# Half of a gate product moved into the opening of an RWKV-7 scan, with the scan's first loads reordered

## The chip, the cores and the metric

The kernel runs on 1 core of one Trainium2 chip. The metric is the device time of one execution in microseconds. Lower is better.

## The reference

Two encoder layers on x (512 tokens, 1024 channels, float32). Each is a half-step SwiGLU feed-forward, a token mixer, and another half-step feed-forward, with a layer norm after each. Layer 0 mixes by neighbourhood attention, layer 1 by bidirectional RWKV-7. Only the second mixer matters here:

```
xr, xw, xk, xv, xa, xg = (x + xx * mix[i] for i in range(6))
r = xr @ w_rkv[0];  k = xk @ w_rkv[1];  v = xv @ w_rkv[2]
decay, a = low-rank functions of xw and xa, one per direction
g = sigmoid(xg @ g1) @ g2                      # 1024 -> 160 -> 1024
state_t = state * w_t + (state a_t) b_t + v_t k_t ;  y_t = state r_t      # 16 heads of 64, both directions
out = ((groupnorm(y) + bonus) * g) @ w_out
```

## The kernel before, in words

Everything is laid out with channels (or tokens) on 128 partitions. Products that need accuracy are made of three float32r passes (`mm3`, lines 226 to 230: high x high, high x low, low x high); a product given plain float32 tiles is a single call.

**rwkv_project** (lines 582 to 750) makes the mixer's inputs. Near its end it opens the first scan pool (`scan.begin`), makes the decays of both directions, and the gate: `rank(0)` and `rank(0, g1b)` are g1's product in plain float32 (line 614), tanh makes the sigmoid, `split` cuts it into high and low halves `gh`. Then, for each of eight chunks of 128 output channels, six float32r passes (`mm3` for 128 and for 32 rows of g2), a copy by ACT (`store`, line 643) and a store into the DRAM tile `g` (line 644). Between the chunks runs `scan.front(0, 0)`, the preparation of head pair 0 in the forward direction.

**Scan** works through eight pairs of heads in slots -2 to 7. A slot holds generator threads, and the string `SEQ[n]` says in which order their steps are written: f0, f1 are `front` of a direction (decay sums, line 1266; exponents; rank product; tanh; then DVE's products into ar and bk), g0, g1 `grams` (line 1324, masked by DVE at 1329, with swaps by DMA at 1336 and 1337), t0, t1 `tails`, v `values` (weights wv loaded at line 1356, then eight products with xv, two matmul halves each by `wide`, line 1015), r `receptances`, l `load`, i, k, j the inversion, c the chain over the chunks of time (lines 1474 to 1494), d outputs, b bonus. PE, ACT and DVE keep exactly this order (`manual_schedule(MANUAL_SCAN)`). SP, which issues all DMAs, and POOL are put in order by a scheduler from when each instruction would be ready; after that every queue runs in order.

**receptances** (lines 1083 to 1120) loads the eight chunks of xr into the buffers az[2], xs8 and xs9, then the receptance weights of pairs 1, 4, 6, 7 (`WR_FIRST`; the first goes into xs4), with the eight chunks of xv between, then three more weights into vt. The products alternate between the PSUM banks y and m, one buffer each, and are copied into the tiles yt and yh, one buffer each. The loads are written at the first step of r, in slot -2.

The scan's large pool and a second one (`open`, line 1044) lie over the memory of the pools that rwkv_project closes: the rings that hold gh and the copies to be stored, and the weight tiles that hold g2.

Of the kernel before, what the change touches and what calls it, by code (L numbers as in the profile page):

```python
# [10 lines left out]
F32 = mybir.dt.float32  # L11
# [3 lines left out]
AF = mybir.ActivationFunctionType  # L15
# [3 lines left out]
P = 128  # L19
D = 1024  # L20
S = 512
FF = 2816
NF = FF // P
ND = D // P
# [18 lines left out]
CH = 64  # L43
# [15 lines left out]
}  # L59
SEQ = {  # L60
# [11 lines left out]
}  # L72
EARLY = 5
START_TAGS = ("k", "iv", "r", "lw", "kz0", "ar0", "bk0", "a2r", "a2u", "pcs")
EARLY_TAGS = ("kz1", "v", "vr", "qc", "qd", "zs", "qs", "tm")
DECAY = math.exp(-0.5)
GN_EPS = 64e-5
# [22 lines left out]
class Trunk:  # L100
# [481 lines left out]
    def rwkv_project(self, dram, xraw, w_rkv, w1, w2, a1, g1, g2, heads, xs, scan):  # L582

        nc = self.nc
        if True:
# [77 lines left out]
            with self.tc.manual_schedule(engines=MANUAL):  # L663
# [62 lines left out]
                            nc.sync.dma_start(dram["lw"][:, z, t, ws], th)  # L726

                xs.close()
                scan.begin()
                decays(0)  # L730
                scan.fetch(0, 0)
                pg = [rank(0), rank(0, g1b)]
                gn = (P, 32)
                for i, n in enumerate(gn):
                    raw = self.tmp()[:n]
                    nc.scalar.activation(raw, pg[i][:n], AF.Tanh, scale=0.5)
                    nc.vector.tensor_scalar(raw, raw, 0.5, 0.5, ALU.mult, ALU.add)
                    self.split(gh[i][:n, 0, :], gh[i][:n, 1, :], raw)
# [2 lines left out]
                start = scan.front(0, 0)  # L741
                next(start)
                ug = [self.load_rows(g2, 0), self.load_unit(g2[P:, :])]
                for c in range(ND):
                    pp = self.bank()
                    for i, n in enumerate(gn):
                        cs = slice(c * P, c * P + P)
                        self.mm3(pp, ug[i][:n, 0, cs], ug[i][:n, 1, cs], gh[i][:n, 0, :], gh[i][:n, 1, :], i == 0, i == 1)
                    store(dram["g"][:, c, :], pp)
                    next(start, None)  # L750

    def rwkv_out(self, acc, params, lead):
        self.spare.append(self.ring())
# [256 lines left out]
class Scan:  # L1010
# [10 lines left out]
        self.free = list(range(NBUF))  # L1021
        self.taken, self.st, self.py = {}, {}, {}

    def begin(self):

        nc = self.nc
        pool = self.start = self.opened.enter_context(self.k.pool("rws", "right"))
        self.tri = pool.tile([P, 2, P], F32, name="tri")
        self.mask = pool.tile([P, 2, 2, CH], F32, name="mask")
        self.onesb = pool.tile([P, P], F32, name="onesb")  # L1030
        self.ah = pool.tile([P, 2, S], F32R, name="ah")
        ring = self.k.ring(F32)
        raw, *rest = (ring[:, i * S : (i + 1) * S] for i in range(4))
        self.first.update(zip(("e", "e2", "th"), rest))
        for dst, src in ((raw, self.dram["ah"]), (self.tri, self.consts["tri"])):
            nc.sync.dma_start(dst, src)
        load = self.load(0)
        next(load)
        self.k.split(self.ah[:, 0, :], self.ah[:, 1, :], raw)
        next(load)  # L1040
        for n in ("mask", "onesb"):
            nc.sync.dma_start(getattr(self, n), self.consts[n])

    def open(self, pool):

        self.pool = pool
        early = self.early = self.opened.enter_context(self.k.pool("rwe", "right"))
        self.eye = self.consts["eye"]
        self.xv = pool.tile([P, ND, S], F32, name="xv")
        unit = lambda i: (pool.tile([P, 2, 4, 2, CH], F32, name=f"xs{i}"), pool.tile([P, 2, 4, CH], F32, name=f"tb{i}"))  # L1050
        units = {i: unit(i) for i in (2, 4, 3)}
        for n in ("e", "e2", "th"):
            self.place(n, [P, S], 2)
        for n in ("yt", "yh"):
            self.place(n, [P, S])
        self.place("bon", [P, S], 2)
        self.place("gate", [P, S])
        units.update({i: unit(i) for i in (7, 0, 9, 1)})
        self.place("vt", [P, NC, 2, 2, CH], 2)
        units.update({i: unit(i) for i in (5, 6, 8)})  # L1060
        self.units = [units[i] for i in range(NBUF)]


        self.az = [pool.tile([P, 2, NU, CH], F32, name=f"az{i}") for i in range(3)]
        for i in range(2):
            self.clear(i)
        self.room(0)
# [4 lines left out]
    def tile(self, tag, shape, bufs=1, dtype=F32):  # L1072
        if tag in self.first:
            return self.first.pop(tag)
        pool = self.start if tag in START_TAGS else self.early if tag in EARLY_TAGS else self.pool
        return pool.tile(shape, dtype, name=tag, tag=tag, bufs=bufs)

# [5 lines left out]
    def receptances(self):  # L1083

        nc = self.nc
        one = lambda ap: ap.rearrange("p a b c d -> p (a b c d)")
        az = self.az[2].rearrange("p a b c -> p (a b c)")
        xr = [h[:, i * S : (i + 1) * S] for h, n in ((az, 4), (one(self.units[-2][0]), 2), (one(self.units[-1][0]), 2)) for i in range(n)]
        for c in range(ND):
            nc.sync.dma_start(xr[c], self.dram["xr"][:, c, :])  # L1090
        w = {}

        def load(hp, ap):
            w[hp] = ap.rearrange("p (c f) -> p c f", c=ND)
            nc.sync.dma_start(w[hp], self.w_r[:, hp * P : (hp + 1) * P].rearrange("(c p) f -> p c f", p=P))

        for hp, i in zip(WR_FIRST, (4, 5, 6, 7)):
            load(hp, one(self.units[i][0]))
            if hp == 1:
                for c in range(ND):  # L1100
                    nc.sync.dma_start(self.xv[:, c, :], self.dram["xv"][:, c, :])
        rest = [hp for hp in range(1, ND) if hp not in WR_FIRST]
        order = WR_FIRST + tuple(rest)
        while rest:
            pair, rest = rest[:2], rest[2:]
            vt = self.tile("vt", [P, NC, 2, 2, CH], 2)
            for i, hp in enumerate(pair):
                load(hp, one(vt)[:, i * D : (i + 1) * D])
        for i, hp in enumerate(order):
            pr = self.k.bank("ym"[i % 2])  # L1110
            for c in range(ND):
                self.wide(pr, w[hp][:, c, :], xr[c], c == 0, c == ND - 1)
                if c % 2 and c < ND - 1:
                    yield
            t = self.tile(("yh", "yt")[hp % 2], [P, S])
            nc.scalar.activation(t, pr, AF.Copy)
            nc.sync.dma_start(self.dram["rkv"][0][:, hp, :], t)
            if hp == order[-1]:
                self.clear(2)
            yield  # L1120
# [9 lines left out]

    def run(self, late, lead, ln):
        with self.k.tc.manual_schedule(engines=MANUAL_SCAN):
            self.zs = []
            for _ in range(2):
                self.unit()
            self.rs, self.out = self.receptances(), self.outs()
            self.led, self.stored = [], 0
            for n in range(-2, HEADS // 2):
                if n == HEADS // 2 - 1:
                    self.early.tile([P, 56], F32, name="pad")  # L1140
                    self.opened.close()
                    late.enter_context(self.k.early())
                    self.lw = self.leads(lead, ln)
                self.slot(n)
            self.ending = self.finish(HEADS // 2 - 1)
            next(self.ending)
# [59 lines left out]
    def slot(self, n):  # L1206
# [3 lines left out]
            ("t0", "tails", n + 2, 0), ("t1", "tails", n + 2, 1), ("v", "values", n + 2), ("b", "bonus", n + 2),  # L1210
            ("e", "gate", n - 1), ("x", "finish", n - 1), ("n", "turn", n + 1), ("i", "invert", n + 2), ("k", "inverted", n + 1), ("j", "merge", n + 1),
            ("l", "load", n + 3), ("c", "chain", n), ("d", "outputs", n))}
        threads["r"], threads["o"] = self.rs, self.out
        threads["w"] = self.lw if n == HEADS // 2 - 1 else iter(())
        for name in SEQ.get(n, SEQ[0]).split():
# [8 lines left out]
    def load(self, hp):  # L1224

        k, nc, tile_ = self.k, self.nc, self.tile
        p = self.st[hp] = Pair()
        p.k, p.iv = (tile_(n, [P, S], 2) for n in ("k", "iv"))
        nc.sync.dma_start(p.k, self.dram["rkv"][1][:, hp, :])
        for h in range(2):  # L1230
            nc.sync.dma_start(p.iv[HALF[h]], self.dram["iv"][2 * hp + h : 2 * hp + h + 1, :].broadcast_to([CH, S]))
# [21 lines left out]
    def front(self, hp, z):  # L1253
# [2 lines left out]
        p = self.st[hp]  # L1256
        way = slice(None, None, -1) if z else slice(None)
        if z == 0:
            p.r = tile_("r", [P, S], 2)
            nc.sync.dma_start(p.r, self.dram["rkv"][0][:, hp, :])  # L1260
        if (hp, z) not in self.lws:
            self.fetch(hp, z)
# [88 lines left out]
    def values(self, hp):  # L1351

        k, nc, tile_ = self.k, self.nc, self.tile
        p = self.st[hp]
        wv = tile_("wv", [P, ND, P])
        nc.sync.dma_start(wv, self.w_v[:, hp * P : (hp + 1) * P].rearrange("(c p) f -> p c f", p=P))
        yield
        p.v = tile_("v", [P, S], 2)
        pv = k.bank("a")
        for c in range(ND):  # L1360
            self.wide(pv, wv[:, c, :], self.xv[:, c, :], c == 0, c == ND - 1)
            if c < ND - 1:
                yield
        nc.scalar.activation(p.v, pv, AF.Copy)
        yield

    def bonus(self, hp):
        k, nc, tile_ = self.k, self.nc, self.tile
# [379 lines left out]
```

## Time and profile before

| what | us |
|---|---|
| median of 3 runs | 2245.5 (2244.44 to 2251.05) |
| the profiled execution | 2242.69 |
| its span, first to last instruction | 2240.9 |
| PE busy | 2175.0 (97% of the span) |
| POOL, DVE, ACT busy | 1411.7, 1060.0, 958.0 |

The profile follows one execution. Times in its rows are microseconds from the start of the span unless marked ns. PE is TensorE, DVE VectorE, ACT ScalarE, POOL GpSimd, SP the engine that issues DMAs. A DMA row gives the time of its issue, not of its transfer. PE's matmuls overlap, so a row's duration is longer than its distance to the next. What stands in brackets behind a row is the idle time of its engine before it and the instruction or transfer that ended it. The granted clock is the share of TensorE's full 2.4 GHz.

### The profile page before, as it was taken

Reading aid. Unit: us, or ns where it says so; the run is one execution under the profiler, and the core shown is the slowest. Engines: PE = TensorE matmul, PEld = TensorE weight load, DVE = VectorE, ACT = ScalarE, POOL = GpSimd, SP = SyncE. Lnnn points to the kernel's source line nnn. Section 1 sums busy time; section 2 is a strip of 40 time slices with the busy share of each in tenths; the row PEclk is TensorE's granted clock in tenths of the full one; section 3 lists DMA queues with packets and bytes.
Section 4 is the critical chain, followed back from the end, with each engine's and each line's share of the span. In section 5 each row is a group of like instructions: output and inputs, shape, how many; then the busy total and the mean of one; then the engine's idle time right before and its main releaser. Section 6 shows DMA issues by size and latency. Waiting matters only on the chain. (4 is left out here: it accounts for less than half of the span.)

```text
span 2240.9 us, 35205 instructions
## 1 busy us (share of the span) xinstructions
PE 2175.0 (97%) x13850; PEld 1706.6 (76%) x13850; DVE 1060.0 (47%) x1524; ACT 958.0 (43%) x1678; POOL 1411.7 (63%) x1234
## 2 busy tenths in 40 slices
PE   8999999999999999999999999799999899999998
PEld 7888888887888888888888875345666557888886
DVE  2333355377432333633333588234788545333345
ACT  3333345376343333443333444336777533333333
POOL 6877855554488786588787432044676712888754
PEclk9999999999999999999999999899999999999999
DMA  6444462432344444454444546844544643544443
GB/s 200 141 142 150 146 230 97 126 91 88 109 139 142 149 146 160 141 188 141 137 141 141 197 128 214 249 123 130 135 121 118 191 152 98 161 140 137 141 169 122
DMA packets 350497, 328.82 MB, mean 147 GB/s; under 512 B 48458, under 2 KB 277450, under 8 KB 350332
## 3 DMA queue, kind: packets, MB, share of 16 engines
q1 hardware_dynamic: 350332, 326.58, 47.1%
q8 instruction: 109, 1.79, 0.3%
q14 instruction: 56, 0.46, 0.1%
HBM read 262.26 MB, written 47.74 MB: 138 GB/s over the span
## 5 line engine op out<-in xcount | busy, mean ns | idle before, releaser
L224 POOL TENSOR_TENSOR w<-raw,w 128x1024 fp32r<-128x1024 f32 x200 | 492.0, 2461 | 246.5 <-ACT w L223 241.7
L228 PE MATMUL bank<-xT,w 128*128 128x512 f32 x1408 | 549.3, 390 | 0.0
L229 PE MATMUL bank<-xT,w 128*128 128x512 f32 x1408 | 548.0, 389 | 0.0
L230 PE MATMUL bank<-xT,w 128*128 128x512 f32 x1408 | 547.9, 389 | 0.0
L223 ACT ACTIVATE w<-raw 128x1024 fp32r<-128x1024 f32 (+1 forms) x204 | 215.3, 1058 | 329.2 <-POOL ts L794 138.0
L430 DVE SCALAR_TENSOR_TENSOR ar<-bank,tmp 128x512 f32<-128x512 f32 x88 | 60.9, 692 | 583.7 <-PE bank L230 574.7
L230 PEld LDWEIGHTS bank<-xT,w 128*128 128x128 f32 x1408 | 264.3, 188 | 55.0
L228 PEld LDWEIGHTS bank<-xT,w 128*128 128x128 f32 x1408 | 264.3, 188 | 54.0
L229 PEld LDWEIGHTS bank<-xT,w 128*128 128x128 f32 x1408 | 264.4, 188 | 53.6
L823 PE MATMUL bank<-wx,an 128*128 128x512 f32 x792 | 187.3, 389 | 0.0
L1413 POOL TENSOR_TENSOR tm<-qs,zs 128x126 f32<-128x126 f32 (+22 forms) x248 | 104.5, 421 | 115.9 <-DVE qs L1406 66.2
L823 PEld LDWEIGHTS bank<-wx,an 128*128 128x128 f32 x792 | 148.7, 188 | 30.9
L823 PE MATMUL bank<-w,ring 128*128 128x512 f32 x720 | 168.7, 390 | 2.0 <-POOL w L224 2.0
L224 POOL TENSOR_TENSOR wx<-ra,wx 128x512 fp32r<-128x512 f32 x132 | 166.8, 1291 | 3.1 <-ACT wx L223 3.1
L224 DVE TENSOR_TENSOR ring<-ar,ring 128x1024 fp32r<-128x1024 f32 x44 | 129.5, 2943 | 75.5 <-ACT ring L223 75.4
L823 PEld LDWEIGHTS bank<-w,ring 128*128 128x128 f32 x720 | 135.0, 188 | 31.2 <-POOL w L224 2.9
L428 ACT ACTIVATE tmp<-bank 128x512 f32<-128x512 f32 x88 | 52.6, 598 | 229.2 <-PE bank L230 229.1
L224 POOL TENSOR_TENSOR ring<-raw,ring 128x1024 fp32r<-128x1024 f32 x28 | 68.4, 2449 | 103.6 <-ACT ring L223 98.9
L1415 POOL TENSOR_TENSOR zs<-zs,tm 128x126 f32<-128x126 f32 (+22 forms) x248 | 112.9, 455 | 19.4
L223 ACT ACTIVATE wx<-ra 128x512 fp32r<-128x512 f32 x132 | 82.9, 633 | 72.0 <-PE bank L823 67.9
L224 POOL TENSOR_TENSOR w<-late,w 128x1024 fp32r<-128x1024 f32 x30 | 75.3, 2511 | 60.0 <-ACT w L223 59.9
L228 PE MATMUL bank<-xT,ring 128*128 128x256 f32 (+1 forms) x352 | 102.1, 298 | 5.0 <-ACT ring L223 2.2
(295 smaller groups left out, 3752.1 us busy)
## 6 DMA issues: line engine op xcount, KB each, us to landing
raw<-in_ffn_w_in_dram SPq DMA_DIRECT2D x176, 512.0 KB, 3.9
ra<-in_ffn_w_out_dram SPq DMA_DIRECT2D x44, 1024.0 KB, 5.0
late<-d_late SPq DMA_DIRECT2D x34, 512.0 KB, 5.4
late<-in_ffn_w_out_dram SPq DMA_DIRECT2D x28, 512.0 KB, 4.4
raw<-in_w_qkv_dram SPq DMA_DIRECT2D x24, 512.0 KB, 3.9
d_late<-ts SPq DMA_DIRECT2D x44, 256.0 KB, 3.4
d_late<-ra SPq DMA_DIRECT2D x44, 256.0 KB, 2.0
xs<-ar SPq DMA_DIRECT2D x64, 128.0 KB, 2.4
```

What stands on the lines that cost most here:

```text
L223: self.hi = self.nc.scalar.activation(h, raw, AF.Copy).ins
L224: self.lo = (eng or self.nc.vector).tensor_tensor(l, raw, h.bitcast(F32), ALU.subtract).ins
L228: nc.tensor.matmul(out, wh, xh, start=start, stop=False)
L229: nc.tensor.matmul(out, wh, xl, start=False, stop=False)
L230: nc.tensor.matmul(out, wl, xh, start=False, stop=stop)
L428: nc.scalar.activation(s, pg, AF.Silu)
L430: nc.vector.scalar_tensor_tensor(raw[:, 3:7:3] if j else raw[:, 0:8:7], halves_of(pu), 0.5, halves_of(s), ALU.mult, ALU.mult)
L823: self.nc.tensor.matmul(acc, lhs, u[:, i], start=bool(first) and m == 0, stop=last and m == 2, skip_group_check=more)
L1413: nc.gpsimd.tensor_tensor(tv, qs[:, s, 0:s].rearrange("p (a o) -> p a o", o=1).broadcast_to([P, s, n]), zs[:, s : s + 1, c0:].broadcast_to ...
L1415: nc.gpsimd.tensor_tensor(zs[:, 0:s, c0:], zs[:, 0:s, c0:], tv, ALU.add)
```

## The change

Four of the gate's eight chunks (`GATES`) stay where they were. The other four become a thread q, written at the start of slot -2, between the steps of `front(0, 1)` and ahead of the first Grams; they are plain float32 products of the unsplit sigmoid (`hidden`, 128 and 32 rows) with the second half of g2, loaded into the start pool by `begin`. They use the banks y and m and the tiles yh and yt. `hidden` and that part of g2 afterwards hold k, iv and r of the odd pairs; the even pairs get single tiles. mask and onesb are loaded behind, in another pool. The receptances' loads get another order, and their first part is written ahead of the slots. Values' weights are loaded at the end of the values thread before, and in `SEQ[0]` the first product step of values moves from before the chain's fourth step to after the next pair of chain steps.

```
 SEQ[-2]
-    "g0 v f1 f1 f1 f1 f1 f1 g0 l g0 r r g0 g0 v r g1 ...
+    "f1 q q f1 q f1 q g0 v f1 f1 f1 g0 l g0 r r g0 g0 v r g1 ...
 SEQ[0]
-    "c f1 x f1 v c n c f1 f1 v c g0 c c d f1 c n c d g0 l ...
+    "c f1 x f1 v c n c f1 f1 c g0 c c d v f1 c n c d g0 l ...
+GATES = 4
-START_TAGS = ("k", "iv", "r", "lw", ...
+START_TAGS = ("k0", "iv0", "r0", "lw", ...
 rwkv_project
-                scan.begin()
+                scan.begin(g2)
...
-                    raw = self.tmp()[:n]
+                    raw = scan.hidden[:n, i, :]
...
-                for c in range(ND):
+                for c in range(ND - GATES):
...
-                    next(start, None)
+                    next(start)
+                list(start)
 Scan.begin
-        self.mask = pool.tile([P, 2, 2, CH], F32, name="mask")
-        self.onesb = pool.tile([P, P], F32, name="onesb")
+        self.hidden, self.g2 = (pool.tile([P, 2, S], F32, name=n) for n in ("gh", "g2"))
+        self.fixed = dict(zip(("k1", "iv1", "r1"), (self.hidden[:, 0], self.hidden[:, 1], self.g2[:, 0])))
+        for i, n in enumerate((P, 32)):
+            nc.sync.dma_start(self.g2[:n, i, : GATES * P], g2[i * P : i * P + n, (ND - GATES) * P :])
...
-        for n in ("mask", "onesb"):
-            nc.sync.dma_start(getattr(self, n), self.consts[n])
 Scan.open
+        self.mask = early.tile([P, 2, 2, CH], F32, name="mask")
+        self.onesb = early.tile([P, P], F32, name="onesb")
 Scan.receptances
-        for c in range(ND):
-            nc.sync.dma_start(xr[c], self.dram["xr"][:, c, :])
...
+        def chunk(c):
+            nc.sync.dma_start(xr[c], self.dram["xr"][:, c, :])
+
+        for n in ("mask", "onesb"):
+            nc.sync.dma_start(getattr(self, n), self.consts[n])
+        chunk(0)
         for hp, i in zip(WR_FIRST, (4, 5, 6, 7)):
             load(hp, one(self.units[i][0]))
-            if hp == 1:
+            if hp == WR_FIRST[0]:
+                for c in range(1, ND):
+                    chunk(c)
+                self.weigh(0)
+                yield
                 for c in range(ND):
                     nc.sync.dma_start(self.xv[:, c, :], self.dram["xv"][:, c, :])
+        for _ in range(2):
+            self.unit()
 Scan.run
-            self.zs = []
-            for _ in range(2):
-                self.unit()
-            self.rs, self.out = self.receptances(), self.outs()
+            self.zs, self.rs, self.out = [], self.receptances(), self.outs()
+            next(self.rs)
 Scan.slot
+        threads["q"] = self.gates() if n == -2 else iter(())
 Scan.load, Scan.front
-        p.k, p.iv = (tile_(n, [P, S], 2) for n in ("k", "iv"))
+        p.k, p.iv = (tile_(f"{n}{hp % 2}", [P, S]) for n in ("k", "iv"))
-            p.r = tile_("r", [P, S], 2)
+            p.r = tile_(f"r{hp % 2}", [P, S])
 Scan.values
-        wv = tile_("wv", [P, ND, P])
-        nc.sync.dma_start(wv, self.w_v[:, hp * P : (hp + 1) * P].rearrange("(c p) f -> p c f", p=P))
+        wv = self.wv
...
         nc.scalar.activation(p.v, pv, AF.Copy)
+        self.weigh(hp + 1)
         yield
+    def weigh(self, hp):
+        if self.has(hp):
+            self.wv = self.tile("wv", [P, ND, P])
+            self.nc.sync.dma_start(self.wv, self.w_v[:, hp * P : (hp + 1) * P].rearrange("(c p) f -> p c f", p=P))
+    def gates(self):
+        nc = self.nc
+        for j, c in enumerate(range(ND - GATES, ND)):
+            pg = self.k.bank("ym"[j % 2])
+            for i, n in enumerate((P, 32)):
+                nc.tensor.matmul(pg, self.g2[:n, i, j * P : (j + 1) * P], self.hidden[:n, i, :], start=i == 0, stop=i == 1)
+            t = self.tile(("yh", "yt")[j % 2], [P, S])
+            nc.scalar.activation(t, pg, AF.Copy)
+            nc.sync.dma_start(self.dram["g"][:, c, :], t)
+            yield
```

## Rows read from the trace of the kernel before

**Rows 1.** The page's first lines: the span, and PE's busy time, share and instructions.
```profile
span 2240.9 us, 35205 instructions
PE 2175.0 (97%) x13850; PEld 1706.6 (76%) x13850; DVE 1060.0 (47%) x1524; ACT 958.0 (43%) x1678; POOL 1411.7 (63%) x1234
```

**Rows 2.** Busy time by window around the scan's opening: start and end, length, then busy us and number of instructions of each engine, the granted clock, the share of the DMA engines' time and GB/s. The engines come in the order PE, PE's weight loads, DVE, ACT, POOL.
```profile
1400.00:1420.00 20.00, 20.00 (x73) 11.00 (x72) 7.78 (x16) 11.14 (x21) 0.00 (x0) 1.00 0.71 231
1420.00:1440.00 20.00, 10.86 (x54) 6.50 (x54) 7.35 (x12) 7.63 (x17) 2.07 (x4) 0.86 0.72 211
1440.00:1450.00 10.00, 2.98 (x8) 1.14 (x10) 0.00 (x0) 0.00 (x0) 0.00 (x0) 0.50 0.99 330
1450.00:1460.00 10.00, 10.00 (x65) 4.18 (x62) 2.58 (x4) 2.25 (x8) 0.00 (x0) 0.92 1.14 297
```

**Rows 3.** PE's timeline in the opening, right behind the gate loop: start, duration, line, operation, tiles, count.
```profile
1427.90 1.16 PE L1324 MATMUL g<-ar,bk 64*128 64x128 f32 x16
...
1430.46 0.40 PE L230 MATMUL a<-ah,a2u 128*128 128x512 f32 x1
1447.02 5.94 PE L1015 MATMUL y<-az,xs 128*64 128x512 f32 x16 [16.16 <-DMA xs<-in_w_rkv_dram]
```

**Rows 4.** Waits from 1425 to 1460: who waited for whom, us in total, times, longest.
```profile
POOL az L1081 <- DMA d_g<-ring: 27.2, 1, 27.2
...
PE y L1015 <- DMA xs<-in_w_rkv_dram: 16.2, 1, 16.2
```

**Rows 5.** SP's timeline: start and length of each run of DMA issues (az and xs from d_xr are the chunks of xr, xs from in_w_rkv the receptance weights, k at 1399.95 belongs to pair 1).
```profile
1399.95 0.44 SPq L1229 DMA_DIRECT2D k<-d_k  x1
...
1429.01 0.42 SPq L1356 DMA_DIRECT2D wv<-in_w_rkv_dram  x1
1429.53 0.71 SPq L1090 DMA_DIRECT2D az<-d_xr  x1
...
1431.74 1.57 SPq L1090 DMA_DIRECT2D az<-d_xr  x3
1436.62 1.13 SPq L1337 DMA_DIRECT2D xs<-ar  x2
1437.79 2.23 SPq L1090 DMA_DIRECT2D xs<-d_xr  x4
1440.07 0.43 SPq L1095 DMA_DIRECT2D xs<-in_w_rkv_dram  x1
```

**Rows 6.** PE's timeline later in slot -2: sixteen receptance matmuls at full clock.
```profile
1464.07 3.65 PE L1015 MATMUL m<-az,xs 128*64 128x512 f32 x16
```

**Rows 7.** PE's timeline before the opening: g1's product in plain float32 (two instructions to a product), three passes of the first gate chunk, the rank product that stands between two chunks, and the chunk after it.
```profile
1392.53 14.01 PE L614 MATMUL bank<-ring 128*128 128x512 f32 x32
...
1412.90 0.48 PE L228 MATMUL bank<-ring,w 128*128 128x512 f32 x1
1413.22 0.40 PE L229 MATMUL bank<-ring,w 128*128 128x512 f32 x1
1413.45 0.40 PE L230 MATMUL bank<-ring,w 128*128 128x512 f32 x1
...
1416.45 0.50 PE L228 MATMUL bank<-ah,a2u 128*128 128x512 f32 x1
...
1417.24 0.40 PE L228 MATMUL bank<-ring,w 128*128 128x512 f32 x1
```

**Rows 8.** DMA issues: tiles, count, KB each, median us from issue to landing; the first for 1415 to 1429, the others for 1429 to 1460.
```profile
d_g<-ring SPq DMA_DIRECT2D x8, 256.0 KB, 3.2
...
xv<-d_xv SPq DMA_DIRECT2D x8, 256.0 KB, 6.9
...
wv<-in_w_rkv_dram SPq DMA_DIRECT2D x1, 512.0 KB, 5.7
```

**Rows 9.** Timelines of ACT and DVE: the copy of a gate chunk, two of the last operations of front(0, 1) on DVE, and the first reading of pair 1's k.
```profile
1420.84 0.60 ACT L643 ACTIVATE ring<-bank 128x512 f32<-128x512 f32 x1 [1.21 <-PE bank L230]
...
1433.19 0.69 DVE L1298 TENSOR_TENSOR kz<-kz,k 128x512 f32<-128x512 f32 x1 [0.88 <-ACT kz L1296]
...
1435.36 0.69 DVE L1302 SCALAR_TENSOR_TENSOR bk<-th,e 128x512 f32<-128x512 f32 x1
...
1487.13 0.96 DVE L1285 SCALAR_TENSOR_TENSOR ar<-k,cols,e 128x504 f32<-128x504 f32 x1
```

**Rows 10.** The end of one slot on PE and SP, and the same place of the next slot on SP: the last value product, and the loads of values' weights.
```profile
1615.95 1.08 PE L1015 MATMUL a<-xv,wv 128*64 128x512 f32 x4
...
1618.22 0.54 SPq L1356 DMA_DIRECT2D wv<-in_w_rkv_dram  x1
...
1656.90 0.97 SPq L1356 DMA_DIRECT2D wv<-in_w_rkv_dram  x1
```

**Rows 11.** PE's waits from 1500 to 1773, slots -1 to 5.
```profile
PE a L228 <- DVE bon L1375: 2.7, 1, 2.7
...
PE a L1015 <- DMA wv<-in_w_rkv_dram: 1.8, 2, 1.0
...
PE a L1015 <- ACT vt L1487: 0.2, 1, 0.2
```

**Rows 12.** One slot's chain between its third and fourth step: the value step on PE, and the second of ACT's two copies into vt, which the fourth step (L1492) reads.
```profile
1622.98 1.08 PE L1015 MATMUL a<-xv,wv 128*64 128x512 f32 x4
...
1623.21 0.27 ACT L1488 ACTIVATE vt<-c 64x128 f32<-64x128 f32 x1
```

More of the change, by code (lines that the diff above doesn't have):

```diff
@@ L73 @@
 EARLY = 5
-START_TAGS = ("k", "iv", "r", "lw", "kz0", "ar0", "bk0", "a2r", "a2u", "pcs")
+GATES = 4
+START_TAGS = ("k0", "iv0", "r0", "lw", "kz0", "ar0", "bk0", "a2r", "a2u", "pcs")
 EARLY_TAGS = ("kz1", "v", "vr", "qc", "qd", "zs", "qs", "tm")
@@ L1022, in __init__, with begin @@
         self.taken, self.st, self.py = {}, {}, {}
-    def begin(self):
+    def begin(self, g2):
         nc = self.nc
@@ L1074, in tile @@
             return self.first.pop(tag)
+        if tag in self.fixed:
+            return self.fixed[tag]
         pool = self.start if tag in START_TAGS else self.early if tag in EARLY_TAGS else self.pool
```

4 rows, old and new, of the table SEQ are left out of this document.

## The prediction

> **What bounds the kernel now.** I read the page's first line for the whole, then one stretch: its windows, PE's timeline, the waits, and SP's queue. PE is busy 97% of a span of 2240.9 us [rows 1], so a gain has to be PE work removed or one of the few PE stalls closed. The windows [rows 2] show the largest stall of the second layer: PE busy 10.86 of 20 us from 1420, 2.98 of 10 us from 1440, while the DMA engines run at 0.72 and 0.99 of their time. PE's timeline [rows 3] places it: behind the gate loop come the opening's first Grams (L1324) at 1427.90, decay sums and a rank product (to L230), and from about 1430.86 PE waits 16.16 us for the receptance weights. The wait list names one transfer [rows 4]. SP's queue [rows 5] says why it was so late: values' weights at 1429.01, eight xr chunks between 1429.53 and 1440, a block before 1436.62 behind the Grams' swaps, and only at 1440.07 the weights that PE needs first. The stall costs more than its length. The granted clock was 0.50, the 1.2 GHz level, from 1440 to 1450, and the first sixteen receptance matmuls took 5.94 us where sixteen like them took 3.65 at full clock [rows 3, 6]: 2.3 us more.
>
> **The change, part by part.** (a) *Four gate chunks leave the front.* From the first (1412.90) to the first Gram (1427.90) are 15.0 us [rows 3, 7], of which the rank product between chunks took 0.79 (1416.45 to 1417.24 [rows 7]); eight chunks make 14.2 us, 1.78 each. Four removed: the loop ends 7.1 us earlier, at 1420.8.
>
> (b) *Four chunks in plain fp32 come into the opening.* L614 is plain fp32 of the same width: 16 products in 14.01 us [rows 7], 0.876 each, whether 128 or 32 columns of weights. Two a chunk make 1.75, four chunks 7.0. PE's sum of work changes by -0.1 us; the gain can only come from these 7 us standing inside the stall. PE reaches the first receptance again at about 1430.9. Here a rule speaks against the change. In the loop a chunk's six fp32r passes are not dense: starts are 0.32 and 0.23 apart [rows 7], 1.78 for six. *The Trainium skill ("FP8 and Floating Point Precision", TensorE Precision Notes) says true fp32 takes four passes through the array. L614's 0.876 agrees; against three fp32r passes at the loop's closest spacing, 0.23 us, it would make the moved half 1.5 us dearer instead of 0.1 cheaper, and the sum 2237.2.* I take the measured 1.78: it is of the very products removed.
>
> (c) *The first loads.* They write memory of the closing pools; the clear of the neighbouring az waited for a gate store [rows 4]. With the loop over 7.1 us earlier they can start near 1422 instead of 1429. The new order is chunk 0, weights, chunks 1 to 7, value weights. The weights' landing took 6.95 us in the crowded queue (1440.07 to 1447.02 [rows 3, 5]) and value weights, issued into a quieter one, 5.7 [rows 8]; so they land by 1428 to 1430, before PE comes. By data alone the stall would vanish, apart from about 1 us.
>
> (d) *A new wait: the gates' evacuation.* The four products use PSUM banks y and m in turn and the tiles yh and yt in turn, one of each. The third copy (ACT, into yh) must wait until the first store has read yh; the first receptance takes bank y, so PE waits for that third copy. ACT is kept in written order, so the exponent pair passes, but tanh of the second front stands behind the copy as well. The store is issued by SP, and in program order ten loads stand before it that need nothing but free memory: xr 8 x 256 KB, two weights of 512 KB, 3.15 MB. I expect them ahead in the queue, where a ready transfer of earlier program order goes first (load(1)'s k, issued far ahead, shows that readiness counts [rows 5]). With mask, onesb and the store itself it is 3.6 MB from about 1422: at the 330 GB/s of 1440 to 1450 10.9 us, at the 211 GB/s of 1420 to 1440 17.1 us [rows 2]. The bounds are a landing at 1432.9 and 1439.1. In a queue with bulk loads ahead, xv's chunks landed 6.9 us after issue, in a lighter one the gate stores after 3.2 [rows 8]; the store's issue, paced by 0.4 to 0.5 us an issue [rows 5] and by the landings before it, is near 1428.5, giving 1435.4. I take 1436. The copy is 0.60 (L643 [rows 9]), so PE starts at 1436.7: 5.8 us idle, 10.4 less than before. *The Trainium skill ("DMA: Bandwidth & Descriptors", Anatomy of one DMA) puts a transfer's fixed part near 2 us and the rest at bytes over 436 GB/s; by that the store lands 2.6 us after issue, an estimate from that page, and the sum is that of rival A.* The 6.9 us row is nearer, for the queue is full here.
>
> (e) *Clock.* Part of the stall remains, so I keep the 2.3 us loss in full: gain 0, bounds 0 and 2.3.
>
> (f) *What is late next.* The second front's tanh runs at about 1437 behind that copy; its last four operations on DVE take 2.86 us (1433.19 to 1436.05 [rows 9]), so bk is ready near 1442. The Grams g1 stand on PE behind receptance (3.65 to 5.94), Grams (1.1), a value step (0.9) and a receptance step (1.9), past 1444: covered. Value weights and xv chunk 0 land by about 1437, needed past 1441: covered.
>
> (g) *Value weights a slot ahead.* They already are: the load at 1618.22 was issued 1.3 us after the last value product of that slot (1615.95, 1.0 us long), and 1656.90 is the same place a slot later [rows 10]. Nothing moves. What does move is the first value step in slots 0 to 5, from before the chain's fourth step (L1492) to after the next pair. That removes PE's waits on wv, 1.8 us, and 0.2 on vt [rows 11]. It also uncovers a wait: L1492 needs ACT's vt copies, done at 1623.48 in that slot, while PE would be free at 1622.98 [rows 12]: 0.5 us, in five slots (in the first, PE stood 2.7 us on the bonus [rows 11], with the copies done). 2.6 added, 2.0 removed: +0.6, bounds -2.0 and +3.
>
> (h) *Small edits.* mask and onesb move behind, g2's last half (256 and 64 KB) comes into the start: within 1400 to 1420 PE was busy 20.00 of 20 us [rows 2], and nothing there waits on a transfer. k, iv and r of the odd pairs reuse the gate's tiles; pair 1's k and iv load after the fourth gate product, near 1430 instead of 1400 [rows 5], and k is first read at 1487.13 [rows 9]: hidden by 40 us. If that cover were gone, 0.5 MB at 211 to 330 GB/s, 1.6 to 2.4 us.
>
> Sum: -0.1 - 10.4 + 0.6 = -9.9. The profiled execution took 2242.69 us, so it would take 2232.8; the median of runs stands 2.8 above it at 2245.5, and on that the forecast is 2235.6, rounded to **2236**.
>
> **The rivals.** *A: the store's wait does not bite* (it lands within 3.2 us, as in the light queue, or stands ahead of the loads). Then about 1 us of stall stays and the clock holds: 15.2 + 2.3 + 0.1 - 0.6 = 17.0, 2228.5. For it: the bytes are needed only later. Against: 3.15 MB are ready ahead of it. *B: the order is not realised*: SP issues as before, weights after all xr chunks. Then only the 7.1 us earlier start counts: PE starts near 1440, gain 7.1 - 0.6 = 6.5, 2239. For it: the queue's order is the scheduler's, not the text's; against: the new text puts the weights second. *C: slower.* The stores fall behind xv and the other weights too. At 297 to 330 GB/s [rows 2] xv's 2.1 MB take 6.4 to 7.1 us, each further weight of 512 KB 1.6 to 1.8: behind xv and three weights the store lands near 1448, PE waits 2 us longer than before and the slots add 0.6; behind all six, near 1453, 7 us longer, so 2253. It decides from a landing after 1446.4, where the copy ends at 1447.0. Against it: the stores come before xv in the text.
>
> **How the numbers follow.** Forecast 0.50, A 0.26, B 0.16, C 0.08. The range goes from A's with another 1.5 us of value waits gone, 2227, to the forecast's with the low transfer rate (PE from 1439.8, 7.2 us gained), 3 us of new slot waits and the 2.4 us of (h): 2245.5 - 0.1 - 7.2 + 3 + 2.4 = 2243.6, taken as 2243; it holds B. A difference of 0.3%, 6.7 us, is about what a measurement can tell: faster means below 2238.8. A wholly (0.26), 0.85 of the forecast (0.42) and an eighth of B (0.02) make 0.70; slower, above 2252.2, is half of C, 0.04; the rest 0.26.
>
> **What would show it.** Right: the loop ends 7 us earlier; eight plain fp32 products of 0.88 us before the first receptance; the weights issued second; PE idle 4 to 8 us before the receptances with ACT's copy as releaser, itself waiting on a store of d_g; L1492 waiting some 0.5 us on vt in slots 1 to 5. Wrong: a wait still put down to xs, a wait for bk at g1, the stall at 0, or a DMA-bound stall later in the opening that gives the gain back.

## The result and the profile after

The changed kernel took **2232.69 us** (median of 6 runs, 2231.76 to 2236.15) against 2244.97 us before (6 runs beside it, 2241.79 to 2251.05): ratio 0.9939, 95% interval 0.9923 to 0.9956. It is 0.6% faster, and the range of 2227 to 2243 held it; the forecast was 2236. The two profiled executions lie closer together than the medians: 2242.69 before, 2233.19 after, 9.5 us, against the 9.9 of the forecast's sum. The steps are checked between these two.

The page after: the span answers to [rows 1], 9.5 us shorter, while PE's busy time grew by 2.7 us.
```profile
span 2231.4 us, 35176 instructions
PE 2177.7 (98%) x13842; PEld 1703.2 (76%) x13842; DVE 1055.5 (47%) x1524; ACT 959.9 (43%) x1678; POOL 1416.4 (63%) x1234
```

Busy time by window, in the columns of [rows 2]. The stretch from 1440 to 1450 is now full for PE, at a granted clock of 0.79 where it was 2.98 us and 0.50; the DMA engines are at 0.96 over the 20 us from 1420 and above 1 behind them, where they were at 0.72 until 1440.
```profile
1400.00:1420.00 20.00, 20.00 (x73) 10.99 (x72) 7.75 (x16) 11.21 (x21) 0.00 (x0) 1.00 0.61 204
1420.00:1440.00 20.00, 12.87 (x50) 5.44 (x52) 4.63 (x8) 4.32 (x9) 2.07 (x4) 0.85 0.96 305
1440.00:1450.00 10.00, 10.00 (x60) 4.01 (x56) 4.06 (x6) 4.15 (x12) 0.00 (x0) 0.79 1.09 302
1450.00:1460.00 10.00, 10.00 (x62) 3.99 (x60) 3.93 (x6) 5.71 (x17) 0.00 (x0) 1.00 1.12 305
```

PE's timeline, answering to [rows 3]. The line numbers have moved: L1281 are the decay sums behind the gate loop, L1393 the gate products, L1339 the Grams, L1017 receptance and values. The stall stands where it stood before, but it is 7.13 us long, and its releaser is ACT's third gate copy, not a load.
```profile
1420.77 1.16 PE L1281 MATMUL a<-tri,lw 128*128 128x128 f32 x8
1421.76 2.07 PE L1393 MATMUL y<-gh,g 128*128 128x512 f32 x4
1423.77 2.18 PE L1393 MATMUL m<-gh,g 128*128 128x512 f32 x4
1425.87 2.18 PE L1393 MATMUL y<-gh,g 128*128 128x512 f32 x4
...
1428.78 2.07 PE L1393 MATMUL m<-gh,g 128*128 128x512 f32 x4
1430.78 1.16 PE L1339 MATMUL g<-ar,bk 64*128 64x128 f32 x16
1439.07 6.17 PE L1017 MATMUL y<-az,xs 128*64 128x512 f32 x16 [7.13 <-ACT yh L1395]
```

ACT's timeline shows what that copy waited for: ACT stood idle for 10.86 us until the store that reads yh had landed.
```profile
1423.87 0.60 ACT L1395 ACTIVATE yh<-y 128x512 f32<-128x512 f32 x1 [2.40 <-PE y L1393]
...
1438.42 0.60 ACT L1395 ACTIVATE yh<-y 128x512 f32<-128x512 f32 x1 [10.86 <-DMA d_g<-yh]
```

SP's timeline, answering to [rows 5]: chunk 0, weights, seven chunks, value weights (these behind the weights' landing at 1431.14), and then the store, at 1431.90. It landed after 6.4 us, at 1438.31.
```profile
1422.39 0.88 SPq L1431 DMA_DIRECT2D zs<-in_eye_dram  x2
...
1423.79 0.50 SPq L1102 DMA_DIRECT2D az<-d_xr  x1
1424.34 0.42 SPq L1099 DMA_DIRECT2D xs<-in_w_rkv_dram  x1
1424.81 2.06 SPq L1102 DMA_DIRECT2D az<-d_xr  x3
1426.91 2.87 SPq L1102 DMA_DIRECT2D xs<-d_xr  x4
1431.16 0.38 SPq L1385 DMA_DIRECT2D wv<-in_w_rkv_dram  x1
1431.90 0.35 SPq L1396 DMA_DIRECT2D d_g<-yh  x1
```

PE's waits of 1500 to 1773 answer to [rows 11]: no wait on wv is left, a wait on the vt copies (L1519) has come in its place.
```profile
PE a L229 <- DVE bon L1407: 2.7, 1, 2.7
...
PE m L1524 <- ACT vt L1519: 1.7, 7, 0.4
```

Where the 9.5 us are: a mark that comes once in every slot is the first merge product (thread j, `p<-qs,qc`, which joins the halves of the inversion). In slot -1 it starts at 1501.80, 7.72 us earlier than before. Before, then after:
```profile
1509.52 1.20 PE L1446 MATMUL p<-qs,qc 32*32 32x32 f32 x64
```
```profile
1501.80 1.20 PE L1478 MATMUL p<-qs,qc 32*32 32x32 f32 x64
```
The 7.72 are the stall's 9.03 (16.16 less 7.13), less 1.08 by which PE came to it later (1430.86 to 1431.94), less 0.23 for the sixteen receptance products (5.94 to 6.17). The other 1.8 us arose later: the lead is 6.65 us at the same product of slot 0, 9.05 at slot 1's (their distance fell from 41.21 to 38.81 us) and 9.5 at the end; of this, below.

### The profile page after: what moved, and what is told of

Read it like the earlier page. It is cut to its first block, busy times and chain, and to the rows that moved or that the text cites. A ratio compares the mean times of both kernels' runs of the same rounds, so it can differ in the third digit from the quotient of the medians.

```text
span 2231.4 us, 35176 instructions
## 1 busy us (share of the span) xinstructions
PE 2177.7 (98%) x13842; PEld 1703.2 (76%) x13842; DVE 1055.5 (47%) x1524; ACT 959.9 (43%) x1678; POOL 1416.4 (63%) x1234
```

## The experiments

Ten kernels in three rounds, each beside runs of the kernel before (medians 2244.9, 2245.8 and 2245.0). All compute the whole result.

**1. The store's wait alone.** Theory: the wait of step (d) is the stall; rival: the transfers are, and the wait only lies beside them.
```diff
-            t = self.tile(("yh", "yt")[j % 2], [P, S])
+            t = self.tile(("yh", "yt", "gate", "bon")[j], [P, S])
```


> The changed kernel with one thing altered: the third and fourth gate copy write the still unused tiles of the gate and of the bonus instead of using yh and yt a second time, so they no longer wait for the first gate store. Theory (the store's wait is the stall): the changed kernel lost 7.13 us of PE before the first receptance to this wait and about 2.5 us more in the sixteen products behind it, at the lowered clock (6.17 against 3.65). Without it PE reaches the first receptance at 1431.9, the weights landed at 1431.14 and the last xr chunk at 1435.91, so the sixteen products end near 1436.5 instead of 1445.2; next the first value step needs value weights (1437.6) and the first xv chunk (1440.8), which puts up to 4 us of stall back. Sum: 5 us faster than the changed kernel, 2227.5, between 2223 (no new stall) and 2230. Rival (the transfers set the end, the store's wait only lies beside them): PE waits for weights, xr or xv instead, the stall moves and the time stays within 1.5 us of the changed kernel, 2231 to 2234.

2233.17 us, ratio 0.9942 (0.9929 to 0.9955): nothing gained over the changed kernel, outside the theory's 2223 to 2230 and inside the rival's 2231 to 2234. PE's timeline shows the theory's mechanism and the rival's moved stall. The stall before receptance is gone and the sixteen products ran at the full clock, as the theory says; but 6.38 us stand at the first value product. Whether the transfers would set the end in any order, as the rival has it, experiment 6 tells.
```profile
1432.42 3.65 PE L1017 MATMUL y<-az,xs 128*64 128x512 f32 x16 [0.22 <-issue]
1436.01 1.16 PE L1339 MATMUL g<-ar,bk 64*128 64x128 f32 x16
1443.54 1.97 PE L1017 MATMUL a<-xv,wv 128*64 128x512 f32 x4 [6.38 <-DMA xv<-d_xv]
```
Two more gate stores and pair 1's iv, now ready earlier, went ahead of xv chunk 0: issued 1437.19, landed 1443.41, where the changed kernel had 1433.88 and 1440.77. Of these 3.3 us the first store already had 1.2 (issued 1433.06 instead of 1431.90), since the loads began later in this execution; the other 2.1 stand between. The expectation allowed for 4 us of new stall from the old landing and did not ask what the edit itself would push ahead. My size was off by 5.7 us.

**2. The loads' order undone, the gates kept.**
```diff
-        chunk(0)
+        for c in range(ND):
+            chunk(c)
...
-                for c in range(1, ND):
-                    chunk(c)
                 self.weigh(0)
```


> The changed kernel with one thing undone: all eight xr chunks are issued before the first receptance weights again, and the gates stay in the opening. Theory (the store's wait ends last): the weights land some 4 to 5 us later than 1431.14, near 1436, which is still ahead of the gate store's landing at 1438.3, so PE waits for the same copy and the time stays within 1 us of the changed kernel, 2232 to 2233.5: with the store's wait standing, the order of the loads is worth nothing. Rival (the order of the loads is what brought the gain): PE waits for the weights instead, 3 to 5 us more, 2236 to 2238.

2232.45 us (0.9929 to 0.9954), as the theory says. The weights were issued at 1428.92, behind all chunks, and landed at 1435.47, still ahead of the store's landing at 1438.72; the one PE wait of the opening is the same copy:
```profile
PE y L1017 <- ACT yh L1394: 7.6, 1, 7.6
```

**3. The loads' order alone, all gates in the loop.**
```diff
-GATES = 4
+GATES = 0
...
-                    next(start)
+                    next(start, None)
```


> The other half alone: all eight gate chunks stay in the loop as fp32r products, as in the kernel before, and the new order of the first loads and the moved value steps stay. Theory: the loop ends near 1428, the loads start 7 us later than in the changed kernel, PE reaches the first receptance at about 1431 as before, the weights land near 1438 and no store stands in the way: 6 to 8 us of stall instead of 16.16, about the same as the changed kernel, 2233 to 2236. Rival (only products that stand inside the stall bring anything): PE's stall stays above 12 us and the time above 2240.

2236.24 us (0.9943 to 0.9968), 0.2 above the theory's 2233 to 2236: 7.24 us on the weights, and 1.09 that I had not foreseen on xv chunk 0.
```profile
PE y L1017 <- DMA xs<-in_w_rkv_dram: 7.2, 1, 7.2
PE a L1017 <- DMA xv<-d_xv: 1.1, 1, 1.1
```
So of the change's 12.3 us the order alone brings 8.7, the gates without it 12.5, both 12.3. The halves overlap: they shorten the same stall, and either leaves some 7 us of it, on the weights here and on the store there.

**4. The value part undone.**
```diff
-    0: "c f1 x f1 v c n c f1 f1 c g0 c c d v f1 ..."
+    0: "c f1 x f1 v c n c f1 f1 v c g0 c c d f1 ..."
...
+        if hp:
+            self.weigh(hp)
         wv = self.wv
...
-        self.weigh(hp + 1)
```


> The changed kernel with the value part undone: the first value step of slots 0 to 5 before the chain's fourth step again, the value weights loaded at the value step's own start (the first ones still in the opening's order). Step (g) as forecast says that this part costs 0.6 us, so undone it takes 0.6 us less than the changed kernel, 2232.1, with the waits on vt gone and 1.8 us of waits on the value weights back. Rival (the 1.7 us that the changed kernel gained beyond the opening come from this part): 1.7 us more, 2234.4, and the slot from pair -1 to 0 or 0 to 1 is longer by 2.4 us again.

2234.17 us (0.9934 to 0.9961): 1.5 above the changed kernel's median, as the rival has it, but within the spread of either. The distance of the merges of slots 0 and 1 stayed short, 38.72, so the rival's place is ruled out: what the changed kernel gained there does not come from this part. From slot 1's merge to slot 5's it took 155.82 us against 154.45 in the changed kernel, with waits on wv back (0.9) and a wait of 1.6 on ACT's pc. The traces of all ten kernels with the moved step have 153.45 to 154.78 there, so undoing it lies 1.0 us beyond them; but the kernel before, in the order undone to, took 154.19, in their midst. Whether (g) costs 0.6 or saves up to 1.4 is not settled.

**5 and 6. Receptance ahead of values, without and with the four tiles.** The second and third receptance weights go ahead of value weights and xv, six receptance steps ahead of the first value product, load(1) behind.
```diff
-    -2: "... g0 v f1 f1 f1 g0 l g0 r r g0 g0 v r g1 g1 g1 v r g1 v g1 g1 v t0 r g0 r r v f1 b r r t0 v ..."
+    -2: "... g0 f1 f1 f1 g0 g0 r v r l g0 g0 r r r g1 g1 g1 r g1 r g1 g1 r t0 v g0 v v r f1 b v v t0 v ..."
...
-                self.weigh(0)
                 yield
+            if hp == WR_FIRST[2]:
+                self.weigh(0)
                 for c in range(ND):
                     nc.sync.dma_start(self.xv[:, c, :], self.dram["xv"][:, c, :])
```


> The changed kernel with yh and yt still used twice by the gates, but with receptance ahead of values in the opening: the second and third receptance weights are issued before the value weights and xv, and on PE six receptance steps stand before the first value product; load(1) stands behind them. It takes away what made the run with four tiles wait (xv chunk 0 at 1443.4), not the store's wait. Theory (two waits in a row, the store's first): PE still waits for the third gate copy; the value weights no longer stand ahead of the store, so it lands some 1.6 us earlier, near 1436.7, and 5 to 6 us of stall stay; 2230 to 2232.5. Rival (the store's wait only lies beside other transfers, and what ends last is xv): the time falls to that of the run with both edits, 2226 or less.

> Both edits: four tiles for the four gate copies, and receptance ahead of values on the queue and on PE. Theory (two waits in a row, each alone hidden by the other): PE reaches the first receptance at 1432.4 as with four tiles alone, the xr chunks land up to 1437.2 while it works on them, the second weights near 1439 (needed at 1440.4), the first xv chunk near 1443 (needed past 1448); less than 1.5 us of stall in all and no lowered clock, some 8 us less than the changed kernel: 2224.7, between 2222 and 2228. Rival (the queue's throughput sets the end whatever the order): a third wait of 4 us or more, for an xr chunk, the second weights or g1's operands, and 2229 or more.

Without the tiles 2231.51 us (0.9921 to 0.9946), the stall 6.34 us on the same copy:
```profile
1438.06 5.29 PE L1017 MATMUL y<-az,xs 128*64 128x512 f32 x16 [6.34 <-ACT yh L1396]
```
With them **2224.43 us** (0.9894 to 0.9921). PE's timeline of the latter has no stall over 0.24 us left in the opening:
```profile
1429.86 1.16 PE L1340 MATMUL g<-ar,bk 64*128 64x128 f32 x16
1430.95 3.65 PE L1017 MATMUL y<-az,xs 128*64 128x512 f32 x16
...
1439.52 1.94 PE L1017 MATMUL m<-az,xs 128*64 128x512 f32 x8 [0.24 <-DMA xs<-in_w_rkv_dram]
...
1449.61 2.80 PE L1017 MATMUL a<-xv,wv 128*64 128x512 f32 x12
```
And its windows hold the full clock, with the DMA engines about as busy as in the changed kernel (1.06 and 1.09 there):
```profile
1430.00:1440.00 10.00, 9.76 (x67) 4.17 (x69) 5.86 (x9) 4.75 (x12) 0.00 (x0) 1.00 1.08 347
1440.00:1450.00 10.00, 10.00 (x70) 4.42 (x68) 3.93 (x6) 4.54 (x14) 0.00 (x0) 1.00 1.07 312
```
Tiles alone +0.5, order alone -1.2, both -8.3 us against the changed kernel's median; the first two are within the spread of the runs. The traces tell the same without what moves outside the opening: from the loop's end (the first decay sums behind it) to the first merge product of slot -1 it is 81.0 us in the changed kernel, 79.7 with the tiles, 79.4 with the order, 72.1 with both. So there were two waits in a row, each hidden behind the other, and the queue's throughput was not the bound.

**7. The price of the fp32 products.** For each pair of chunks, two products of 128 rows and then two of 32 rows, into banks y and m.
```diff
+            for i, n in enumerate((P, 32)) if j % 2 == 0 else ():
+                for h in (j, j + 1):
+                    pg = banks[h] = banks[h] if i else self.k.bank("ym"[h % 2])
+                    nc.tensor.matmul(pg, self.g2[:n, i, h * P : (h + 1) * P], self.hidden[:n, i, :], ...)
```


> The changed kernel with the gates' fp32 products in another order: two of 128 rows, then two of 32 rows, for each pair of chunks, into banks y and m. In the changed kernel the halves of these products start 0.52 to 0.53 us apart where heights alternate, and 0.43 apart where the first product's second half follows its first; L614's (all of one kind) 0.43. Theory (a change of the weights' height costs the 0.1): half of the changes go, and the eight products take 7.4 us or less instead of 8.1, while PE's start on receptance stays with the store's landing and the time with it, 2232 to 2234. Rival (it is not the height: the reload of weights is simply not hidden for products of this kind): 0.52 everywhere as before, 8.1 us.

One run, 2232.38 us. The same sixteen instructions on PE: 7.55 us, from 1420.88 to 1428.43, where the changed kernel's took 8.2 (three chunks from 1421.76 to 1427.98, and one of 2.0).
```profile
1420.88 1.02 PE L1395 MATMUL y<-gh,g 128*128 128x512 f32 x2
1421.74 1.02 PE L1395 MATMUL m<-gh,g 128*128 128x512 f32 x2
1422.69 1.12 PE L1395 MATMUL y<-gh,g 32*128 32x512 f32 x2
1423.66 1.02 PE L1395 MATMUL m<-gh,g 32*128 32x512 f32 x2
...
1438.43 1.98 PE L1017 MATMUL y<-az,xs 128*64 128x512 f32 x4 [7.95 <-ACT yh L1398]
```
Instruction by instruction, two to a product, the starts stand 0.43 apart as long as the height stays, and 0.52 and 0.53 at the first two instructions behind a change. Of sixteen starts fourteen were late by 0.1 in the changed kernel and seven here; 16 x 0.43 is 6.9, and the late ones make the 8.2 and the 7.55. So the height it is (the rows of weights in a product), 0.2 us for a change of it; the 7.4 that I expected counted one late start for each. The trace of the kernel before has the same in the fp32r passes of its gate loop:
```profile
1417.48 0.40 PE L229 MATMUL bank<-ring,w 128*128 128x512 f32 x1
1417.71 0.40 PE L230 MATMUL bank<-ring,w 128*128 128x512 f32 x1
1418.04 0.49 PE L228 MATMUL bank<-ring,w 32*128 32x512 f32 x1
1418.38 0.39 PE L229 MATMUL bank<-ring,w 32*128 32x512 f32 x1
```
The two starts behind the change are 0.33 and 0.34 apart, the one before it 0.23. It is not the change of operands: the pass at 1417.24 [rows 7] has other operands than the rank product's last pass at 1417.01, and the same height, and follows by 0.23. The time saved went into a longer stall, 7.95 us.

**8. Experiment 6's order with all gates in the loop** (experiments 3 and 5 together, without the tiles, which are then not needed).
```diff
-GATES = 4
+GATES = 0
```


> The order of e6_tiles_and_order on queue and PE, but with all eight gate chunks in the loop as fp32r, as before the change. Theory: loads start 7 us later, so PE waits 7 us for the first receptance weights as in the run with the order alone (7.24), but not for xv behind them (1.09): 2234.5 to 2236, and its distance to e6_tiles_and_order, 8 to 11 us, is what the moved gates are worth once nothing else takes their place. Rival: the moved gates are worth their 7 us only on paper, and this run lies within 3 us of e6_tiles_and_order.

2233.35 us (0.9927 to 0.9952), 1.2 under the theory's range, with 6.88 us on the weights and no wait for xv:
```profile
1437.24 5.18 PE L1017 MATMUL y<-az,xs 128*64 128x512 f32 x16 [6.88 <-DMA xs<-in_w_rkv_dram]
```
The distance to experiment 6 is 8.9 us: that is what the moved gates are worth once no store and no xv takes their place. In the change as it stands they are worth 3.6 (experiment 3 against it).

**9. The stores from ACT's queue.**
```diff
-            nc.sync.dma_start(self.dram["g"][:, c, :], t)
+            nc.scalar.dma_start(self.dram["g"][:, c, :], t)
```


> The changed kernel with the four gate stores issued by ACT's own queue, right behind each copy, instead of by SP behind the ten loads; yh and yt are still used twice. It tells whether the first store landed at 1438.31 because it was issued late, behind the loads in SP's order (issue 1431.90), or because any transfer of that stretch takes 6.4 us. Theory (SP's order): issued near 1424.4, when the loads have just begun, it lands 3 to 5 us later, by 1429.5; the third copy does not hold PE, and the wait for xv chunk 0 takes its place as in the run with four tiles (6.4 us near 1443): 2231 to 2234.5. Rival (the engines are full, whatever the queue): it lands past 1433, and PE waits 3 us or more at the first receptance.

One run, 2226.88 us. It shows the theory's mechanism, not its time. Issued at 1423.02, the first store took 5.3 us and landed at 1428.33; the third copy held nobody, and xv chunk 0 was the wait, 4.2 us:
```profile
PE a L1017 <- DMA xv<-d_xv: 4.2, 1, 4.2
```
The first store's row in the DMA issues of this run, of the changed kernel and of experiment 2 (the last number is us from issue to landing):
```profile
d_g<-yh ACTq DMA_DIRECT2D x1, 256.0 KB, 5.3
```
```profile
d_g<-yh SPq DMA_DIRECT2D x1, 256.0 KB, 6.4
```
```profile
d_g<-yh SPq DMA_DIRECT2D x1, 256.0 KB, 8.4
```
So it was its place behind the loads, with an issue 7.4 us behind the end of the copy in the changed kernel, that made the store late; the time from issue to landing differs by 1.1 us only. The place counts more than the time of the issue: in experiment 2, with the same ten loads ahead, the store was issued at 1430.31, 1.6 us earlier than in the changed kernel, and landed 0.4 later. The time is 4 us under my range: xv chunk 0 was issued at 1432.46 rather than 1437.19 as in experiment 1, and the loop ended 1.5 us earlier in this execution (L1281 at 1419.29) for causes ahead of the opening.

**10. Experiments 6 and 7 together:** the diffs of 1, 5 and 7 in one kernel.

> e6_tiles_and_order with the gates' products paired by height as in e7_products_paired. There the pairing took some 0.7 us off the eight products and nothing off the time, since PE only waited longer; here PE stands on no wait in the opening, so the 0.7 us should come out: 2223.7, which the timing can't tell from e6_tiles_and_order (2224.4), but the start of the first receptance can: some 0.7 us earlier. Rival: the weights or the xr chunks are then late by as much, and PE waits that much longer.

**2222.16 us** (0.9876 to 0.9909), the fastest here; the interval overlaps that of experiment 6. From the first gate product to receptance it took 9.53 us (1420.21 to 1429.74) against 10.11 (1420.84 to 1430.95): the pairing brings 0.6, the rest of the difference is not told apart from an earlier end of the loop.

## Why the prediction was right, step by step

**(a) holds.** The loop ended at 1420.77; the forecast said 1420.8.

**(b) was mis-sized by 1.2 us.** I took L614's 0.876 a product, a row whose products are all of 128 rows of weights. The four chunks, alternating 128 and 32, took 2.0 to 2.1 each instead of 1.75, 8.2 us instead of 7.0. Experiment 7 gives the cause: I set a row without the changes of height against the loop's 1.78 a chunk, which holds them. Like for like, sixteen starts at 0.43 are 6.9 us and twenty-four at 0.23 are 5.5; the late starts add 1.3 to the one (fourteen) and 1.6 to the other (sixteen), which makes 8.2 against 7.1. The term cost nothing, since PE then waited anyway. *The Trainium skill's four passes for true fp32 ("FP8 and Floating Point Precision", TensorE Precision Notes) had made the moved half 1.5 us dearer in the prediction. The trace agrees: 6.9 less 5.5 is 1.4, and 1.1 with the late starts.*

**(c) holds in mechanism, and with the gates moved was worth nothing.** The weights were issued second and landed at 1431.14, about 1 us later than forecast, because two zs and one lw load went first. Experiment 2 shows that the order could as well have stayed: rival B, priced at 2239, came out at 2232.45. Its price took over the old blockade by the Grams' swaps, [rows 5], which the later Grams had already removed: in experiment 2 the first swap was issued at 1439.31, behind the loads.

**(d) is the step that made the forecast.** The copy, the tile, the bank, the releaser and the order on SP are as written; the landing of 1438.31 is inside 1432.9 to 1439.1. The stall is 7.13 us, not 5.8: the store was issued at 1431.90, not 1428.5, since chunk 0 was issued at 1423.79, not near 1422, and the value weights ahead of the store waited 1.4 us for a landing. The landings show a rule behind this that I did not have: in all twelve traces SP issued no transfer before the one eight places ahead had landed (some 680 in each whose landing is recorded), and in the changed kernel's opening 16 of 23 within 0.15 us behind it. The value weights (1431.16) came behind the receptance weights (1431.14), the store (1431.90) behind the second chunk (1431.84). Whether the program or the chip asks for it, no run tells. *The Trainium skill's fit ("DMA: Bandwidth & Descriptors", Anatomy of one DMA), by which I estimated 2.6 us, is given there for transfers that GpSimd issues; these stores, issued by SP and ACT into a full queue, took 6.4 us and, issued early, 5.3.* From 1420 to 1440 the queue moved 305 GB/s, between the 211 and 330 from which the bounds were made.

**(e) holds but for 0.2 us.** The sixteen products took 6.17 us at the lowered clock, and 3.65 at the full one in experiments 1 and 6.

**(f) was right for a reason that hides an error.** xv chunk 0 landed at 1440.77, not by 1437. In the changed kernel it is covered (needed at 1446.27), but only by the store's wait. Rival A, priced at 2228.5 on the premise that no other wait is near, came out at 2233.17. The right price of A needed one more question: with PE 7 us earlier, what does it need next, and when is that issued?

**(g)** showed the waits it named: those on wv went, and L1492's successor L1524 waited 1.7 us in seven places on the vt copies (forecast 2.6 in five; five times 0.5 is 2.5). Its sum is not settled (experiment 4).

**(h) holds.** PE was busy for 20.00 of the 20 us from 1400, and pair 1's k, issued at 1433.25, landed at 1439.95 and was first read at 1479.4.

**That the sum came so near is luck.** The steps up to (f) forecast a gain of 10.5 us and the opening gave 7.7; (g) forecast a loss of 0.6 and the slots gave 1.8.

**What I did not have: what slots 0 and 1 gave.** The kernel before waits 1.98 us at slot 0's first merge product for qs, made from POOL's result; the changed kernel 0.3. It goes with the granted clock, not with the change. In the changed kernel the clock falls behind the 2.66 us stall near 1535, so PE comes later and finds qs ready; in experiment 1 it holds there, PE waits for qs, and the clock falls behind that wait. The twelve traces show no third outcome: in three (the kernel before, experiments 1 and 2) the granted clock is 1.00 over the 8 us behind the stall, qs is waited for 1.6 to 2.0 us, and the merges of slots 0 and 1 lie 41.2 to 41.5 us apart; in the other nine it is 0.59 to 0.79, the wait 0.5 us at most, and the distance 38.5 to 38.9. Windows of the changed kernel, then of experiment 1:
```profile
1530.00:1540.00 10.00, 7.34 (x87) 5.86 (x85) 9.01 (x19) 4.52 (x11) 8.59 (x17) 0.83 0.50 156
1560.00:1570.00 10.00, 9.62 (x196) 6.25 (x198) 8.17 (x14) 7.67 (x22) 5.88 (x15) 1.00 0.21 37
```
```profile
1530.00:1540.00 10.00, 7.34 (x101) 5.13 (x101) 8.72 (x17) 5.25 (x13) 8.67 (x18) 1.00 0.50 147
1560.00:1570.00 10.00, 8.38 (x135) 6.13 (x133) 7.70 (x12) 4.90 (x13) 5.97 (x14) 0.66 0.25 52
```
From slot -1's merge to slot 1's it is 101.11 us in the one and 103.43 in the other. Which of the two comes, no run here explains. It is a caution for reading single executions, as are the 1.8 us by which the loop's end moves between them (from 1419.22 to 1421.03 in the kernels with moved gates).

## What to carry to other kernels

Before a stall is priced as removed, write down the next two things its engine needs and when each is issued: here two waits of 6 to 7 us stood one behind the other, each edit alone gave about 1 us or nothing, both together 8.3. A small buffer used twice across a store is here a wait on the ten loads queued ahead of that store; two more tiles, already allocated and idle, remove it. Work moved into a stall is worth its full time only once the stall's other causes are gone: the same four chunks were worth 3.6 us with the store's wait and 8.9 us without it.

## What the runs showed of the hardware

A product whose weights have another height than the ones before it costs 0.2 us more, whichever way the height changes between 128 and 32 rows: two starts are late by 0.1, in plain fp32 (0.52 and 0.53 apart instead of 0.43) and in fp32r passes (0.33 and 0.34 instead of 0.23). And the first gate store, 256 KB, took 5.3 us issued by ACT at 1423.02, 6.4 by SP at 1431.90, and 5.6 to 8.4 in the eight kernels that issue it from SP, with the DMA engines at 0.9 of their time and more, against 3.2 in the lighter stretch of [rows 8] (0.54 from 1415 to 1429): what the other queue changed was mainly when the store was issued, not how long it ran. Last, no transfer was issued before the one eight places ahead had landed, in any of the twelve traces; in experiment 9 this holds for SP and ACT counted together.
